# Multiply and tanh-GELU in two stretches of DRAM instead of three, with one multiply of 2048 columns on GpSimd

## The chip, the core and the metric

The kernel runs on one core of a Trainium2 chip. The metric is the device time of one execution in microseconds. Three runs of the kernel before took 119.83, 119.99 and 120.62 us; the median is 119.99.

## What is computed

Two arrays of 1024 x 4096 float32 (16.78 MB each) are multiplied element by element, and the product goes through the tanh form of GELU. The result has the same shape and type.

```python
z = x * y
return (0.5 * z * (1 + np.tanh(np.sqrt(2 / np.pi) * (z + 0.044715 * z ** 3)))).astype(np.float32)
```

Every element is independent of every other, so any cut of the arrays will do as long as x, y and the result are cut alike.

## The kernel before

The arrays are treated as flat memory. Split over the 128 partitions of SBUF, each array has 32768 columns of 4 bytes in every partition. The list `PIECES` (line 14) cuts the flat memory into three stretches, of 1280, 16384 and 15104 columns for each partition. Within a stretch, partition p holds one run of contiguous memory; `columns` (line 51) makes that view. So a row of a transfer, which is what one partition gets, is 5,120, 65,536 or 60,416 bytes of contiguous DRAM.

All of x stays in SBUF (`xs`, line 61, 128 KB for each partition). y does not fit beside it and has a smaller buffer, `ys` with `Y_BUF` = 20440 columns, in which later parts of y overwrite earlier ones. `Y_LOADS` (line 16) holds for each load of y its first and last column and its place in the buffer; `Y_FREE` (line 18) how many multiplies must be done before that load may be issued.

Everything in DRAM is moved by transfers that SyncE (SP) issues into one queue, in program order: x piece 0 and x piece 1 (moved by `_hoist` to the very front of the program), y load 0 (columns 1280 to 17664), x piece 2, then, after the third multiply, y load 1 (17664 to 32768), and after the fourth, y load 2 (0 to 1280). After these come three stores in the order of `STORES`. The first waits for y load 1 to have landed, and each waits for the activations of its own columns (lines 112 and 113). The waits stand in SP's program, so a wait that is not over holds back every later issue.

VectorE (DVE) multiplies in place, `xs = xs * ys` (line 96): four steps of 4096 columns, seven of 2048, one of 768 and one of 1280, as `STEPS` has them. It waits for the x and y that a step reads (lines 92 and 93), and each multiply adds one to `sem_mul`. ScalarE (ACT) applies the GELU in place (line 104), one activation for each multiply and in the same order; it waits for that multiply and adds one to `sem_act`. GpSimd (POOL) does no work of the kernel. At the end SP waits for the first two stores, clears the semaphores, and waits for the last store.

Of the kernel before, what the change touches and what calls it, by code (L numbers as in the profile page):

```python
# [1 line left out]

# [4 lines left out]


F32 = mybir.dt.float32
GELU = mybir.ActivationFunctionType.Gelu_apprx_tanh  # L10

PIECES = [(0, 1280), (1280, 17664), (17664, 32768)]

Y_LOADS = [(1280, 17664, 4056), (17664, 32768, 0), (0, 1280, 15104)]

Y_FREE = [0, 3, 4]

STEPS = [[4096] * 4, [2048] * 7 + [768], [1280]]  # L20
STORES = [(1280, 17664), (17664, 32768), (0, 1280)]
Y_BUF = 20440


def _hoist(nc, issued):

    here = nc.cur_bb.bb.instructions
    first = nc.main_func.blocks[0].instructions
    for ins in issued:
        del here[next(k for k, i in enumerate(here) if i is ins or i.name == ins.name)]  # L30
    engine = issued[0].engine
    at = next(
        k
        for k, i in enumerate(first)
        if i.engine == engine and type(i).__name__ == "InstDrain"
    )
    first[at:at] = issued


@with_exitstack  # L40
def kernel(
    ctx: ExitStack,
    tc: tile.TileContext,
    x: bass.AP,
    y: bass.AP,
    out: bass.AP,
):
    nc = tc.nc
    P = nc.NUM_PARTITIONS

    def columns(t, a, b):

        flat = t.flatten_outer_dims().rearrange("r c -> (r c)")
        pa, pb = next(q for q in PIECES if q[0] <= a and b <= q[1])
        return flat[P * pa : P * pb].rearrange("(p c) -> p c", p=P)[:, a - pa : b - pa]


    tc.close()
    tc.compile()  # L59

    xs = nc.alloc_sbuf_tensor("xs", [P, PIECES[-1][1]], F32).ap()
    ys = nc.alloc_sbuf_tensor("ys", [P, Y_BUF], F32).ap()
    sem_x = [nc.alloc_semaphore(f"sem_x{i}") for i in range(len(PIECES))]
    sem_y = [nc.alloc_semaphore(f"sem_y{i}") for i in range(len(Y_LOADS))]
    sem_mul = nc.alloc_semaphore("sem_mul")
    sem_act = nc.alloc_semaphore("sem_act")
    sem_o = [nc.alloc_semaphore(f"sem_o{i}") for i in range(len(STORES))]

    def load_x(i):
        a, b = PIECES[i]  # L70
        return nc.sync.dma_start(out=xs[:, a:b], in_=columns(x, a, b)).then_inc(sem_x[i], 16)

    def load_y(i):
        a, b, r = Y_LOADS[i]
        return nc.sync.dma_start(
            out=ys[:, r : r + b - a], in_=columns(y, a, b)
        ).then_inc(sem_y[i], 16)

    _hoist(nc, [load_x(0).ins, load_x(1).ins])
    load_y(0)  # L80
    load_x(2)
    for i in range(1, len(Y_LOADS)):
        if Y_FREE[i]:
            nc.sync.wait_ge(sem_mul, Y_FREE[i])
        load_y(i)

    n = 0
    done = {}
    for i, (a, b, r) in enumerate(Y_LOADS):
        for j, (xa, xb) in enumerate(PIECES):  # L90
            if xa <= a < xb:
                nc.vector.wait_ge(sem_x[j], 16)
        nc.vector.wait_ge(sem_y[i], 16)  # L93
        c = a
        for w in STEPS[i]:
            nc.vector.tensor_mul(  # L96
                out=xs[:, c : c + w],
                in0=xs[:, c : c + w],
                in1=ys[:, r + c - a : r + c - a + w],
            ).then_inc(sem_mul, 1)  # L100
            n += 1
            done[c + w] = n
            nc.scalar.wait_ge(sem_mul, n)
            nc.scalar.activation(  # L104
                out=xs[:, c : c + w], in_=xs[:, c : c + w], func=GELU
            ).then_inc(sem_act, 1)
            c += w

    for i, (a, b) in enumerate(STORES):
        if i == 0:  # L110
            nc.sync.wait_ge(sem_y[-2], 16)
        nc.sync.wait_ge(sem_act, done[b])
        nc.sync.dma_start(out=columns(out, a, b), in_=xs[:, a:b]).then_inc(sem_o[i], 16)
    for i in range(len(STORES) - 1):
        nc.sync.wait_ge(sem_o[i], 16)
    nums = sorted(s.num for s in [*sem_x, *sem_y, *sem_o[:-1], sem_mul, sem_act])
    assert nums == list(range(nums[0], nums[-1] + 1))
    nc.sync.sem_clear(range(nums[0], nums[-1] + 1))
    nc.sync.wait_ge(sem_o[-1], 16).then_inc(sem_o[-1], -16)


# [1 line left out]
_INS = ['x', 'y']  # L123
_OUTS = [((1024, 4096), 'float32')]


# [23 lines left out]
```

## Time and profile before

| what | value |
|---|---|
| median of three runs | 119.99 us |
| the profiled execution, its own time | 119.64 us |
| its span, first to last instruction | 118.3 us |
| HBM read, written | 33.55 MB, 16.78 MB |
| DVE busy | 35.2 us, 13 multiplies |
| ACT busy | 31.0 us, 13 activations and one table load |
| POOL busy | 0.2 us, four memsets |

The profile is that of one execution. Its span starts with the first instruction, SP's issue of x piece 0, and ends with SP's last wait; the time of the execution is 1.34 us longer. A row of the groups of instructions gives line, engine, operation, output and input with their shapes and count, then the busy time in us and the mean duration in ns, then the idle time ahead of the group and what ended it. The DMA bar cuts the span, or a window of it, into 40 equal slices; each digit is the share of the 16 DMA engines' time that was busy in a slice, in tenths. In a narrow window of that view a packet is put down where it starts, so that it shows the starts and not the busy time. The first half of the work begins on DVE at 42.45 us and the second at 78.12, each when a load of y has landed:

```profile
42.00:60.00 18.00, 17.43 (x4) 10.94 (x4) 0.00 (x0) 1.00 0.99 430
60.00:78.00 18.00, 0.00 (x0) 3.53 (x1) 0.00 (x0) 1.00 0.90 391
```

This is the table of windows: the stretch in us and its length, the busy time of DVE, ACT and POOL with the number of instructions, the granted TensorE clock (not used here), the DMA share, and GB/s.

### The profile page before, as it was taken

The page shows a single profiled execution, that of the slowest core. Times are in us where ns is not written, and L with a number is a line of the kernel's source. Part 1 is how long each engine was busy: PE and PEld are TensorE (multiplying, and loading weights), DVE is VectorE, ACT ScalarE, POOL GpSimd, SP SyncE. Part 2 cuts the span into 40 slices and gives each one's busy share as a digit, 9 for nine tenths or more (in the row PEclk, how much of TensorE's full clock was granted, in tenths as well). Part 3 has the DMA queues.
Part 4 walks back from the last instruction along what each step waited for, and adds up shares of the span by engine and source line. Part 5 has one row for each costly group of instructions (what it writes and reads, how often), then busy time and mean ns, then how long its engine had stood idle before and what let it go on. Part 6 is the DMA issues. An engine that isn't in the chain of part 4 may idle for free.

```text
span 118.3 us, 82 instructions
## 1 busy us (share of the span) xinstructions
DVE 35.2 (30%) x13; ACT 31.0 (26%) x14; POOL 0.2 (0%) x4
## 2 busy tenths in 40 slices
DVE  0000000000000069999920000059999940000000
ACT  3000000000000001977974000007998990000000
POOL 0000000000000000000000000000000000000000
DMA  9988899889988897797797797798899888977975
GB/s 375 556 355 355 355 643 421 355 355 421 643 355 355 355 654 327 327 654 327 327 654 327 327 654 327 327 576 355 355 576 487 355 355 368 613 327 327 654 327 222
DMA packets 1296, 50.33 MB, mean 425 GB/s; under 512 B 144, under 2 KB 144, under 8 KB 528
## 3 DMA queue, kind: packets, MB, share of 16 engines
q1 hardware_dynamic: 1296, 50.33, 98.8%
HBM read 33.55 MB, written 16.78 MB: 425 GB/s over the span
## 4 chain that ended last, share of the span: by engine, by line
DMA 53%; DVE 24%; ACT 3%; issue 1%; DVEq 0%
DMA ys<-in_y_dram 53%; DVE xs L96 24%; ACT xs L104 3%; DVEq L93 0%
## 5 line engine op out<-in xcount | busy, mean ns | idle before, releaser
L96 DVE TENSOR_TENSOR xs<-xs,ys 128x2048 f32<-128x2048 f32 (+3 forms) x13 | 35.2, 2778 | 60.7 <-DMA ys<-in_y_dram 60.7
L104 ACT ACTIVATE xs<-xs 128x2048 f32<-128x2048 f32 (+3 forms) x13 | 29.7, 2301 | 64.5 <-DVE xs L96 64.5
L104 ACT ACT_TABLE_LOAD x1 | 1.3, 1283 | 1.9 <-PEq L59 1.9
L134 POOL MEMSET const-bfloat16-1.0<- 128x1 bf16 x1 | 0.1, 102 | 0.0
L134 POOL MEMSET const-uint8-127<- 128x1 uint8 x1 | 0.1, 102 | 0.0
L134 POOL MEMSET const-float32-0.0<- 128x1 f32 x1 | 0.1, 99 | 0.2 <-issue 0.2
L134 POOL MEMSET const-float32-1.0<- 128x1 f32 x1 | 0.1, 99 | 0.0
## 6 DMA issues: line engine op xcount, KB each, us to landing
xs<-in_x_dram SPq DMA_DIRECT2D x1, 7552.0 KB, 57.9
ys<-in_y_dram SPq DMA_DIRECT2D x1, 7552.0 KB, 22.5
out_dram<-xs SPq DMA_DIRECT2D x1, 7552.0 KB, 20.4
xs<-in_x_dram SPq DMA_DIRECT2D x1, 640.0 KB, 3.6
ys<-in_y_dram SPq DMA_DIRECT2D x1, 640.0 KB, 19.7
out_dram<-xs SPq DMA_DIRECT2D x1, 640.0 KB, 20.8
xs<-in_x_dram SPq DMA_DIRECT2D x1, 22.6
ys<-in_y_dram SPq DMA_DIRECT2D x1, 40.4
```

Source lines behind the costliest of these rows:

```text
L96: nc.vector.tensor_mul(out=xs[:, c : c + w], in0=xs[:, c : c + w], in1=ys[:, r + c - a : r + c - a + w],).then_inc(sem_mul, 1)
L104: nc.scalar.activation(out=xs[:, c : c + w], in_=xs[:, c : c + w], func=GELU).then_inc(sem_act, 1)
L134: nc = _bacc.Bacc("TRN2", target_bir_lowering=False, num_devices=1)
```

## The change

The stretches of DRAM become two, of 16384 columns each, so that all views of DRAM have a distance of 64 KB from row to row. What is loaded is cut apart from them: x as columns 0 to 1280 (heads of the rows of stretch 0, 5 KB each), 1280 to 16384 and 16384 to 32768; y as 0 to 16384, 16384 to 31488 and, as tails of the rows of stretch 1, 31488 to 32768. There are two stores, one for each stretch, each with rows of 64 KB, and the last columns no longer have a store to themselves.

The first half is multiplied in four steps of 4096 columns, as before. The second half is cut into nine: 1024, 2048 and 2048 columns, then 2048 that GpSimd multiplies, then the tail of 1280, three of 2048 and one of 1792. GpSimd has a semaphore of its own, `sem_pool`. ACT takes the steps in the order of the list, GpSimd's as the fourth of the second half. A step now waits for every load of x that it touches, and the clear at the end has the new semaphore in its range.

```diff
-PIECES = [(0, 1280), (1280, 17664), (17664, 32768)]
+PIECES = [(0, 16384), (16384, 32768)]
+X_LOADS = [(0, 1280), (1280, 16384), (16384, 32768)]
...
-Y_LOADS = [(1280, 17664, 4056), (17664, 32768, 0), (0, 1280, 15104)]
+Y_LOADS = [(0, 16384, 4056), (16384, 31488, 0), (31488, 32768, 15104)]
...
-STEPS = [[4096] * 4, [2048] * 7 + [768], [1280]]
-STORES = [(1280, 17664), (17664, 32768), (0, 1280)]
+STEPS = [
+    *((0, c, 4096, False) for c in range(0, 16384, 4096)),
+    (1, 16384, 1024, False),
+    (1, 17408, 2048, False),
+    (1, 19456, 2048, False),
+    (1, 21504, 2048, True),
+    (2, 31488, 1280, False),
+    *((1, c, min(2048, 31488 - c), False) for c in range(23552, 31488, 2048)),
+]
+STORES = PIECES
...
+    waited = {nc.vector: set(), nc.gpsimd: set()}
+    muls = {nc.vector: 0, nc.gpsimd: 0}
+    sem_of = {nc.vector: sem_mul, nc.gpsimd: sem_pool}
+    for i, c, w, on_pool in STEPS:
+        engine = nc.gpsimd if on_pool else nc.vector
+        needed = [sem_y[i]] + [
+            sem_x[j] for j, (xa, xb) in enumerate(X_LOADS) if xa < c + w and c < xb
+        ]
+        for sem in needed:
+            if sem.num not in waited[engine]:
+                waited[engine].add(sem.num)
+                engine.wait_ge(sem, 16)
+        a, b, r = Y_LOADS[i]
+        engine.tensor_mul(
+            out=xs[:, c : c + w],
+            in0=xs[:, c : c + w],
+            in1=ys[:, r + c - a : r + c - a + w],
+        ).then_inc(sem_of[engine], 1)
+        muls[engine] += 1
+        nc.scalar.wait_ge(sem_of[engine], muls[engine])
+        nc.scalar.activation(
+            out=xs[:, c : c + w], in_=xs[:, c : c + w], func=GELU
+        ).then_inc(sem_act, 1)
...
-        nc.sync.wait_ge(sem_act, done[b])
+        nc.sync.wait_ge(sem_act, max(n for n, (_, c, _, _) in enumerate(STEPS, 1) if a <= c < b))
```

More of the change, by code (lines that the diff above doesn't have):

```diff
@@ L62 @@
     ys = nc.alloc_sbuf_tensor("ys", [P, Y_BUF], F32).ap()
-    sem_x = [nc.alloc_semaphore(f"sem_x{i}") for i in range(len(PIECES))]
+    sem_x = [nc.alloc_semaphore(f"sem_x{i}") for i in range(len(X_LOADS))]
     sem_y = [nc.alloc_semaphore(f"sem_y{i}") for i in range(len(Y_LOADS))]
     sem_mul = nc.alloc_semaphore("sem_mul")
+    sem_pool = nc.alloc_semaphore("sem_pool")
     sem_act = nc.alloc_semaphore("sem_act")
@@ L69, in load_x @@
     def load_x(i):
-        a, b = PIECES[i]
+        a, b = X_LOADS[i]
         return nc.sync.dma_start(out=xs[:, a:b], in_=columns(x, a, b)).then_inc(sem_x[i], 16)
@@ L85 @@
         load_y(i)
[L87 to L107, printed above, removed]
+    waited = {nc.vector: set(), nc.gpsimd: set()}
[21 more added lines that the diff above has]
+        ).then_inc(sem_act, 1)
     for i, (a, b) in enumerate(STORES):
@@ L115 @@
         nc.sync.wait_ge(sem_o[i], 16)
-    nums = sorted(s.num for s in [*sem_x, *sem_y, *sem_o[:-1], sem_mul, sem_act])
+    nums = sorted(s.num for s in [*sem_x, *sem_y, *sem_o[:-1], sem_mul, sem_pool, sem_act])
     assert nums == list(range(nums[0], nums[-1] + 1))
```

## The prediction

> **What bounds the kernel now.** I read the page's head, its DMA bar and its queue row first.
>
> ```profile
> span 118.3 us, 82 instructions
> DMA  9988899889988897797797797798899888977975
> q1 hardware_dynamic: 1296, 50.33, 98.8%
> ```
>
> The bar never falls to a gap; the queue's packets fill 98.8% of sixteen engines' span. DVE (35.2 us) and ACT (31.0 us) are idle two thirds of it. The kernel ends when 50.33 MB have moved; compute matters only if it leaves the queue empty.
>
> So I looked for unused queue time. At the front, the DMA view of 0 to 4 us (slices of 0.1 us):
>
> ```profile
> DMA  0000000000993956798979799969999990000000
> ```
>
> The first packet starts in the eleventh slice, at about 1.04 us, although SyncE issued at 0.00: **issue to first packet is 1.04 us**. At the end, the issue rows give the three stores' times to landing (the row without a size is the 8,192 KB store), and SyncE's timeline their issues, the last two in windows of their own:
>
> ```profile
> out_dram<-xs SPq DMA_DIRECT2D x1, 7552.0 KB, 20.4
> out_dram<-xs SPq DMA_DIRECT2D x1, 640.0 KB, 20.8
> out_dram<-xs SPq DMA_DIRECT2D x1, 20.9
> ...
> 96.33 0.34 SPq L113 DMA_DIRECT2D out_dram<-xs  x1
> 97.49 0.33 SPq L113 DMA_DIRECT2D out_dram<-xs  x1
> ```
>
> They land at 78.04 + 20.9 = 98.9, 96.33 + 20.4 = 116.7 and 97.49 + 20.8 = 118.3. The DMA view of 98 to 99 us (slices of 25 ns) holds sixteen packets of 60 KB, one for each engine: the second store's first ones.
>
> ```profile
> DMA  0000000000009999999900000000000000000000
> ```
>
> They start between 98.3 and 98.5 us. That is when the engines finish store 0, so **the next store must be issued by 98.3 - 1.04 = 97.3 us** or the queue runs dry. Now it is issued at 96.33: 0.9 us to spare. The work that releases it, the chain of waits and two shape rows:
>
> ```profile
> 78.03 0.03 issue
> 78.06 0.02 DVEq L93
> 78.08 0.04 issue
> 78.12 1.52 DVE xs L96
> 79.64 0.69 issue
> 80.33 13.31 DVE xs L96 x6
> 93.64 0.02 issue
> 93.66 3.80 ACT xs L104 x3
> ...
> L96 DVE TENSOR_TENSOR xs<-xs,ys 128x2048 f32<-128x2048 f32 x7 | 15.5, 2286 | 18.2 <-DMA ys<-in_y_dram 18.2
> L104 ACT ACTIVATE xs<-xs 128x2048 f32<-128x2048 f32 x7 | 13.4, 1910 | 18.7 <-DVE xs L96 18.7
> ```
>
> From the second large y load (78.03) it is DVE back to back, then ACT. The 0.69 us of "issue" is no gap: the first multiply lasts 2.29 us, so it covers them.
>
> **What the Trainium skill says.** "SBUF — State Buffer", Who interferes with whom: a DVE instruction with two SBUF inputs contends with a GpSimd instruction that reads SBUF, since DVE's second input comes through the read interface that both share; the section calls it an exclusive lock, and "SBUF: two separate sides" adds that the later one is blocked until the earlier is through. Every multiply here has two SBUF inputs. The trace before cannot agree or differ: POOL has four memsets, over by 0.5 us. Its other rule, that compute and DMA do not slow each other, fits: while DVE and ACT worked, 80 to 98 us, the DMA share was 0.94. "DMA: Bandwidth & Descriptors", Latency and other measured facts, gives 207 GB/s per direction at a row pitch of 512 KiB, where larger powers of two fall to half; 64 KB is below these. The trace agrees: the large x and y loads of the first 42 us have that pitch and moved at full rate.
>
> **The change, part by part.**
>
> *Transfers.* The bytes stay; nine transfers become eight, and a third of the 384 rows of 5 KB goes. The last store of such rows adds 118.3 - 116.7 = 1.6 us for 0.655 MB; at the stream's 50.33 MB / (118.3 - 1.04 - 0.4) = 431 GB/s it would be 1.52. At most 0.1 us is gained. The x heads at 64 KB pitch are the first packets of all; bounds -0.3 to +0.3 us, since the first stretch to 42.4 us lost 0.4 us against 431 GB/s; I take 0.
>
> *First half.* The first multiply waits for 16.78 MB instead of 17.43: 1.5 us earlier. SyncE's y1 and y2 (waits on the third and fourth multiply) move from 55.57 and 59.91 to some 54.0 and 58.4. The transfer before y1 still ends near 60 (x2 now 2.30 + 57.9 = 60.2), so this slack only grows: worth 0. Three waits ahead of DVE's first multiply cost one 0.02 us event more, hidden by the wait for y0.
>
> *Second half, no contention.* y1 lands after the same bytes, at 78.03; y2 and store 0 queue behind it as before. ACT's starts give the step between DVE multiplies: 2.20 us for 2048 columns, 4.33 for 4096, so 0.07 us + 1.04 ns a column, and a result 0.08 after the next start. ACT takes 0.20 us + 0.83 ns a column, with 0.095 of overlap (1.91 + 0.83 + 1.25 in 3.80). DVE from 78.12: the 1024 columns done at 79.33, then 81.54, 83.74, the 1280 tail at 85.14, and 87.34, 89.54, 91.74, 93.68. **The GpSimd multiply is not in the trace.** The skill's price, "GPSIMD Engine Reference", Elementwise — side-by-side cycle accounting, is 4,497 ns for an fp32 add of 2048 (and 2,293 for DVE, where this trace has 2,286, which lends it weight). I bound a multiply between 2.3 us (DVE's rate) and twice the price, 9 us. At 4.5 it is done at 82.6. ACT takes it fourth, and is not free before 85.6. From there ACT is back to back: 87.5, 88.7, 90.5, 92.3, 94.1, 95.73. Store 1 is issued at 95.75, **1.5 us before the deadline: nothing is lost**. Store 1 now waits for all of its half, without the 1280 columns that a third store took later; were DVE alone to do it, its end at 95.88 would put ACT's at 97.6, 0.3 late.
>
> *Second half, with the lock.* DVE and POOL are released together; nothing in the trace says who starts first, and I let DVE win. Its 1024 columns end at 79.3, POOL runs 4.5 with about 0.1 on each side, DVE resumes at 83.95. The seven left end at 98.37. Behind DVE's multiply stand six more, and behind its wait all of ACT: ACT's fourth to ninth then end at 100.42, store 1 is issued at 100.44, its first packet comes at 101.48, and the sixteen engines have stood still since 98.3 to 98.5: **3.1 us lost**. If POOL wins, the same sum gives 3.0. From 101.48, 8.39 MB at 431 GB/s take 19.5, landing 0.4: span 121.3, where it was 118.3. SyncE's final waits and its clear of the semaphores lie beside the last store. Nothing else stands in POOL's queue.
>
> Bounds of the contention: below, 0 (the queue cannot be fuller than 98.8%); above, POOL held until DVE's last multiply.
>
> **The rivals.**
>
> 1. *Lock, one side held for the other's whole instruction:* +3.0. For it: the skill, and the same shared second input. Against: no measurement here. **0.40.**
> 2. *No loss* (the other side): POOL works beside DVE, or DVE loses less than 1.8 us. Price 0 to -0.1; it decides as long as the store is issued by 97.3, so with POOL done by 87.1 or DVE under about 12% slower. For it: 1.5 us of slack. **0.37.**
> 3. *The interface is shared in turn,* DVE 15 to 25% slower: ACT ends at 97.7 to 99.3, +0.5 to +2.1, I take 1.6. **0.10.**
> 4. *POOL starves* because DVE's multiplies overlap: POOL done at 98.3, ACT stuck at its fourth, end 108.4: +11. **0.10.**
> 5. *Faster by over 1%:* 1.2 us would have to come out of a stream that idles only 1.04 + 0.4 us, neither touched. **0.03.**
>
> That the change doesn't do what it says: its loads and stores are plainly issued so; only POOL's being beside DVE is open, and that is rival 1, 3 or 4.
>
> **The numbers.** The profiled execution took 119.64 us, 1.34 more than its span; the median, 119.99, is 0.35 above it. The likeliest case is the lock: 119.99 + 3.05 = **123.0** (span 121.3, own range 122.3 to 123.6, POOL 3.8 to 5 us). No loss gives 119.9. The range from 119.5 to 123.6 holds rivals 1, 2 and 3 but their fringes, 0.83 in all. Faster by over 1%, 0.03; within 1% (about 1.2 us, what a measurement of this kernel can tell from no change), 0.37; slower, 0.60, from rivals 1, 3 and 4.
>
> **What would show it.** With the lock: store 1 issued near 100.4, zeros in the DMA bar for 3 us after 98.4, DVE idle or one multiply of some 6.5 us near 79 to 84, and POOL's multiply about 4.5 us of work. Right but for the size: the same hole with another width. Wrong: multiplies of 2.29 us on DVE throughout, ACT ending near 95.7, store 1 issued before 97.3 and a closed DMA bar. Starvation: POOL's multiply ending after DVE's last, ACT waiting for it from 85.6.

## The result

The changed kernel takes 122.69 us (median of five runs, 122.60 to 122.95); the kernel before took 119.95 beside it. The ratio is 1.0232, 95% interval 1.0204 to 1.0260: slower by 2.7 us. The forecast was 123.0 with a range of 119.5 to 123.6, and slower as the likeliest side. The profiled execution took 122.60 us, its span is 121.3.

The page of the changed kernel, the lines that answer to those of before:

```profile
span 121.3 us, 82 instructions
...
DMA  6977977977997899779979979699777908897778
...
q1 hardware_dynamic: 1152, 50.33, 96.7%
```

The same 50.33 MB now fill 96.7% of a longer span, and the bar has what it never had before: a 0, in the 33rd slice, which covers 97.0 to 100.1 us. (A packet of 64 KB counts where it starts, and store 0's last ones started at 96.4 to 96.7, so no start falls into that slice though they moved until 99.0; the hole is bounded below with finer views.) The groups of instructions, shapes apart:

```profile
L110 DVE TENSOR_TENSOR xs<-xs,ys 128x2048 f32<-128x2048 f32 x5 | 15.5, 3143 | 0.0
L117 ACT ACTIVATE xs<-xs 128x2048 f32<-128x2048 f32 x6 | 11.1, 1898 | 5.8 <-DVE xs L110 5.8
L110 POOL TENSOR_TENSOR xs<-xs,ys 128x2048 f32<-128x2048 f32 x1 | 5.5, 5542 | 78.3 <-DMA ys<-in_y_dram 78.3
```

DVE's mean for 2048 columns rose from 2286 to 3143 ns. A mean hides which one it was, so here is the timeline (start, duration) from the landing of the second large y load, DVE's second multiply taken by itself from a narrow window, and POOL's:

```profile
78.64 0.35 SPq L125 DMA_DIRECT2D out_dram<-xs  x1
...
78.65 7.74 DVE L110 TENSOR_TENSOR xs<-xs,ys 128x1024 f32<-128x1024 f32 x2 [19.77 <-DMA ys<-in_y_dram]
78.69 5.54 POOL L110 TENSOR_TENSOR xs<-xs,ys 128x2048 f32<-128x2048 f32 x1 [78.26 <-DMA ys<-in_y_dram]
...
79.79 6.60 DVE L110 TENSOR_TENSOR xs<-xs,ys 128x2048 f32<-128x2048 f32 x1
...
86.42 1.91 ACT L117 ACTIVATE xs<-xs 128x2048 f32<-128x2048 f32 x1 [5.46 <-DVE xs L110]
```

One multiply took the whole loss: 6.60 us where the others take 2.28. Neither engine shows as idle; the wait for the other is inside the recorded duration. POOL ends at 78.69 + 5.54 = 84.23 and DVE's long multiply at 79.79 + 6.60 = 86.39, 2.16 us later: nearly all of its own work came after POOL's end. And POOL, recorded from 78.69, worked only from the end of DVE's first multiply (79.88): 4.35 us.

What that does to the store, in SyncE's timeline and the DMA view of 98 to 103 us (slices of 0.125 us, a packet put down at its start):

```profile
100.51 0.34 SPq L125 DMA_DIRECT2D out_dram<-xs  x1
...
DMA  0000000000000000000000000099000000000000
```

Store 1 is issued at 100.51, and its sixteen first packets start between 101.25 and 101.5. Store 0's closing packets, small ones of which each engine has one, lie between 98.9 and 99.1; from 99.1 to 101.2 no packet starts at all. The hole is about 2.4 us.

That is not all of the 3.0 us of span. The second y load landed at 78.63, not 78.03, after the same number of bytes: 0.6 us went earlier, in the loads. The row of DMA issues for the first 640 KB, in the change and then in the kernel before, shows where it begins:

```profile
xs<-in_x_dram SPq DMA_DIRECT2D x1, 640.0 KB, 4.1
```

```profile
xs<-in_x_dram SPq DMA_DIRECT2D x1, 640.0 KB, 3.6
```

The first transfer, now the 5 KB heads at a distance of 64 KB, took 4.1 us to land; the contiguous 640 KB of before took 3.6. The chain of waits shows that nothing more was lost later. Its lines for the two large y loads (start and length, so the sum is the landing), kernel before first:

```profile
1.93 40.42 DMA ys<-in_y_dram
...
55.57 22.46 DMA ys<-in_y_dram
```

```profile
1.91 39.51 DMA ys<-in_y_dram
...
54.57 24.05 DMA ys<-in_y_dram
```

Between the two landings the kernel before takes 35.7 us for 15.47 MB, the change 37.2 us for 16.12 MB: 433 GB/s both times, so the distance of 64 KB does not slow the stream. The 0.6 us is lost ahead of the first landing, which came 0.9 us earlier than before where 0.66 MB less should have brought 1.5.

### The profile page after: what moved, and what is told of

It reads as the page before. It is cut to its first block, busy times and chain, and to the rows that moved or that the text cites. A ratio compares the mean times of both kernels' runs of the same rounds, so it can differ in the third digit from the quotient of the medians.

```text
span 121.3 us, 82 instructions
## 1 busy us (share of the span) xinstructions
DVE 37.3 (31%) x12; ACT 30.6 (25%) x14; POOL 5.7 (5%) x5
## 2 busy tenths in 40 slices
DMA packets 1152, 50.33 MB, mean 415 GB/s; under 512 B 128, under 2 KB 128, under 8 KB 384
## 3 DMA queue, kind: packets, MB, share of 16 engines
q1 hardware_dynamic: 1152, 50.33, 96.7%
## 4 chain that ended last, share of the span: by engine, by line
DMA 52%; DVE 19%; ACT 10%; issue 0%
DMA ys<-in_y_dram 52%; DVE xs L110 19%; ACT xs L117 10%
## 5 line engine op out<-in xcount | busy, mean ns | idle before, releaser
L110 DVE TENSOR_TENSOR xs<-xs,ys 128x2048 f32<-128x2048 f32 (+4 forms) x12 | 37.3, 3176 | 61.2 <-DMA ys<-in_y_dram 61.2
L117 ACT ACTIVATE xs<-xs 128x2048 f32<-128x2048 f32 (+4 forms) x13 | 29.3, 2296 | 68.0 <-DVE xs L110 68.0
L110 POOL TENSOR_TENSOR xs<-xs,ys 128x2048 f32<-128x2048 f32 x1 | 5.5, 5542 | 78.3 <-DMA ys<-in_y_dram 78.3
```

The costliest lines, as they stand in the source:

```text
L110: engine.tensor_mul(out=xs[:, c : c + w], in0=xs[:, c : c + w], in1=ys[:, r + c - a : r + c - a + w],).then_inc(sem_of[engine], 1)
L117: nc.scalar.activation(out=xs[:, c : c + w], in_=xs[:, c : c + w], func=GELU).then_inc(sem_act, 1)
```

## The experiments

**GpSimd taken out of the changed kernel.** Everything else stays, so this divides the loss between GpSimd and the layout.

```diff
-    (1, 21504, 2048, True),
+    (1, 21504, 2048, False),
```

> The changed kernel with GpSimd's multiply given back to DVE, same place in the order, nothing else. Theory (DVE is held for GpSimd's whole multiply): all multiplies of 2048 columns take 2.28 us, the last activation ends near 98.1 us in the span (second y load at 78.65 plus 19.5), store 1 is issued near 98.2 and its first packets come near 99.1, just as the engines finish store 0 (98.9 to 99.1): no hole in the DMA stream or one under 0.3 us. Span 118.9 to 119.3, time 120.2 to 120.7. Rival (the new layout of rows and the two stores cost the time, GpSimd does not): time stays at 122.4 to 122.9.

Measured: 120.49 us, ratio to the kernel before 1.0054 (1.0035 to 1.0073). Its timeline of the second half and the DMA view of 98 to 103 us:

```profile
78.95 17.77 DVE L110 TENSOR_TENSOR xs<-xs,ys 128x1024 f32<-128x1024 f32 x9 [19.77 <-DMA ys<-in_y_dram]
...
98.47 0.34 SPq L125 DMA_DIRECT2D out_dram<-xs  x1
...
DMA  0000000000990000000000000000009900000000
```

DVE does 2048 columns more and is through in 17.77 us, where it took 19.89 with help. Store 1 is issued 19.53 us after the y load instead of 21.87, and its packets start at 99.25 to 99.5 as the engines finish store 0, whose closing packets lie between 99.19 and 99.31: a gap of some 0.15 us is left of the hole. So GpSimd costs 2.0 to 2.2 us (122.69 - 120.49 = 2.2; 2.0 with each taken against the kernel before beside it, 119.95 and 119.75), and the rest of the change about 0.7.

**The multiply on GpSimd where DVE is idle.** The helper stays, and only the place moves: the last 2048 columns of the first half, after DVE's last multiply of that half.

```diff
-    *((0, c, 4096, False) for c in range(0, 16384, 4096)),
+    *((0, c, 4096, False) for c in range(0, 12288, 4096)),
+    (0, 12288, 2048, False),
+    (0, 14336, 2048, True),
...
-    (1, 21504, 2048, True),
+    (1, 21504, 2048, False),
...
+        if on_pool:
+            engine.wait_ge(sem_mul, 4)
```

> GpSimd still multiplies 2048 columns, but those at the end of the first half, and only after DVE's last multiply of that half, when DVE is idle for some 20 us. Theory: GpSimd's multiply takes about 4.4 us, all multiplies of 2048 on DVE take 2.28 us, and the time is that of the kernel without GpSimd (within 0.3 us). Rival (a GpSimd multiply costs the kernel some 2 us wherever it stands, by its start or by slowing DMA): 122 us or more.

Measured: 120.38 us, ratio 1.0050 (1.0032 to 1.0068), the same as without GpSimd. The rows of the two engines:

```profile
L114 DVE TENSOR_TENSOR xs<-xs,ys 128x2048 f32<-128x2048 f32 x7 | 15.7, 2283 | 0.0
...
L114 POOL TENSOR_TENSOR xs<-xs,ys 128x2048 f32<-128x2048 f32 x1 | 4.5, 4507 | 56.7 <-DVE xs L114 56.7
```

Alone, the multiply takes 4.51 us, and no DVE multiply is stretched. So a GpSimd multiply by itself costs this kernel nothing that shows; it costs by standing beside DVE's.

**Which access holds.** Two kernels with all multiplies on DVE give GpSimd an extra instruction on unused columns of `ys` when the y load lands: one fills them (no input), one copies them (one input).

```diff
-    (1, 21504, 2048, True),
+    (1, 21504, 2048, False),
...
+    nc.gpsimd.wait_ge(sem_mul, 4)
+    nc.gpsimd.wait_ge(sem_y[1], 16)
+    nc.gpsimd.memset(ys[:, 16384:18432], 0.0).then_inc(sem_pool, 1)
...
+    nc.sync.wait_ge(sem_pool, 1)
```

> All multiplies on DVE, and GpSimd fills 2048 unused columns of ys with zeros from the moment the second y load has landed: an instruction that writes SBUF and reads nothing, extra work. Theory (the lock is on the shared read interface): no multiply on DVE is longer than 2.3 us, time as the kernel without GpSimd within 0.4 us. Rival (any GpSimd instruction on SBUF holds DVE): one DVE multiply longer by the fill's own duration, some 1.8 us or more, and the end later by about that.

In the second kernel the fill is replaced:

```diff
+    nc.gpsimd.tensor_copy(out=ys[:, 18432:20440], in_=ys[:, 16384:18392]).then_inc(sem_pool, 1)
```

> All multiplies on DVE, and GpSimd copies 2008 unused columns of ys to others from the moment the second y load has landed: one SBUF input, extra work. Theory (an instruction that reads SBUF holds the shared interface for its whole length): one DVE multiply is longer by the copy's working time (some 1.8 to 3 us), and store 1 comes later by that less what slack there is. Rival (DVE and GpSimd share the interface in turn, by bandwidth): several DVE multiplies each longer by some tenths, none doubled; with one input instead of two for GpSimd the loss is at most half of that with the multiply.

Measured, one run each: 120.66 us with the fill, 122.60 with the copy. The fill's rows, then the copy's with DVE's second multiply from the timeline:

```profile
L110 DVE TENSOR_TENSOR xs<-xs,ys 128x2048 f32<-128x2048 f32 x6 | 13.4, 2284 | 0.0
...
L123 POOL MEMSET ys<- 128x2048 f32 x1 | 1.8, 1805 | 78.7 <-DMA ys<-in_y_dram 78.7
```

```profile
L110 DVE TENSOR_TENSOR xs<-xs,ys 128x2048 f32<-128x2048 f32 x6 | 15.0, 2555 | 0.0
...
L123 POOL COPY ys<-ys 128x2008 f32<-128x2008 f32 x1 | 2.8, 2829 | 79.0 <-DMA ys<-in_y_dram 79.0
...
80.45 3.94 DVE L110 TENSOR_TENSOR xs<-xs,ys 128x2048 f32<-128x2048 f32 x1
```

The fill lies beside DVE for 1.8 us and changes nothing. The copy adds six times 2555 - 2284 ns, 1.6 us, to DVE's multiplies. They are one multiply again: its record is 3.94 us, the others keep 2.28. So it is GpSimd's reading that holds DVE, as far as one run of each shows. The copy holds it for less than the multiply, 1.66 against 4.32 us, and a little less than the 1.8 expected at least; from the end of DVE's first multiply (80.54) to its own end (82.25) it has 1.7 us, so the hold is again the length of GpSimd's work. Counted from the y load, store 1 is issued after 21.2 us, where the fill has 19.5 and the change 21.9. The kernel is as late as the change all the same, because its y load landed 0.7 us later in this run.

**Size of the hold.** GpSimd's share is halved.

```diff
-    (1, 21504, 2048, True),
+    (1, 21504, 1024, True),
+    (1, 22528, 1024, False),
```

> The changed kernel, GpSimd's multiply cut to 1024 columns, the other 1024 on DVE. Theory (hold as long as GpSimd's instruction): DVE's second multiply takes 2.28 plus some 2.2 us, store 1 is issued near 99.3, hole about 1.1 us, time about 121.4 to 121.8, near the middle between the change and the kernel without GpSimd. Rival (a fixed cost of starting GpSimd, whatever its size): DVE's second multiply near 6.6 us and the time near 122.5.

Measured: 121.97 us in one run, 0.2 above what was expected at most; its second half began at 79.26, late like the other runs with heads. DVE's second multiply, and SyncE's issue of store 1:

```profile
80.40 4.44 DVE L111 TENSOR_TENSOR xs<-xs,ys 128x2048 f32<-128x2048 f32 x1
...
99.88 0.34 SPq L126 DMA_DIRECT2D out_dram<-xs  x1
```

The stretch is 4.44 - 2.28 = 2.16 us, half of 4.32. From the y load to the store it takes 20.63 us, between 19.53 without GpSimd and 21.87 with 2048 columns. The cost goes with GpSimd's columns; no fixed price for starting it shows.

**Who gets the interface next.** The same 2048 columns as two multiplies.

```diff
-    (1, 21504, 2048, True),
+    (1, 21504, 1024, True),
+    (1, 22528, 1024, True),
```

> The changed kernel, GpSimd's 2048 columns as two multiplies of 1024. Theory (the hold lasts for one instruction, and whoever waits gets the interface next): DVE and GpSimd alternate; two DVE multiplies of 2048 are longer by 2.2 us each (about 4.4 us), the second GpSimd multiply also waits for a DVE multiply and shows 4 us or more; store 1 as late as in the change or some 0.2 us later, time 122.5 to 123.2. Rival (GpSimd keeps the interface as long as it has work queued): one DVE multiply of about 6.7 us and none of 4.4.

Measured: 123.06 us in one run. DVE's third multiply and GpSimd's second, each from a narrow window:

```profile
84.52 4.43 DVE L111 TENSOR_TENSOR xs<-xs,ys 128x2048 f32<-128x2048 f32 x1
...
82.40 4.41 POOL L111 TENSOR_TENSOR xs<-xs,ys 128x1024 f32<-128x1024 f32 x1
```

GpSimd's second multiply begins at 82.40, waits for DVE's second one (which ends at 84.60) and ends at 86.81, with 2.2 us of its own work; DVE's third is stretched for that time. In this run they take turns, an instruction each. DVE loses 2.16 + 2.15 us, as with one long multiply.

**The hold in the kernel before.** Three stretches, three stores, and one step on GpSimd.

```diff
+ON_POOL = [25856]
...
-            nc.vector.tensor_mul(
+            engine, sem = (nc.gpsimd, sem_pool) if c in ON_POOL else (nc.vector, sem_mul)
+            engine.tensor_mul(
...
-            ).then_inc(sem_mul, 1)
+            ).then_inc(sem, 1)
```

> The kernel before with its three stretches and three stores, and only its fifth step of 2048 columns of the second half multiplied on GpSimd. Theory (the hold): DVE's second multiply of the half takes about 6.7 us instead of 2.28 (GpSimd waits for the first, then works 4.5 us), ACT runs back to back from there and ends its twelfth activation near 99.6, store 1 is issued near 99.7 instead of 96.3, first packets near 100.6, a hole of some 2.1 us after 98.4: time 121.6 to 122.1. Rival (without two stores and the new rows GpSimd helps or does nothing): 119.5 to 120.1.

Measured: 121.82 us, ratio 1.0165 (1.0140 to 1.0189). DVE's second multiply and the page's row of GpSimd:

```profile
80.97 6.60 DVE L102 TENSOR_TENSOR xs<-xs,ys 128x2048 f32<-128x2048 f32 x1
...
L102 POOL TENSOR_TENSOR xs<-xs,ys 128x2048 f32<-128x2048 f32 x1 | 6.6, 6607 | 78.4 <-DMA ys<-in_y_dram 78.4
```

The same stretched multiply, the same loss of some 2 us, without two stores and without the new rows. GpSimd's own record is longer here, 6.6 against 5.5 us, only because DVE's first multiply, for which it waits, has 2048 columns and not 1024.

**The layout by itself.** Without GpSimd, x is loaded as two whole stretches, so that no 5 KB heads come first.

```diff
-X_LOADS = [(0, 1280), (1280, 16384), (16384, 32768)]
+X_LOADS = [(0, 16384), (16384, 32768)]
...
-    _hoist(nc, [load_x(0).ins, load_x(1).ins])
+    _hoist(nc, [load_x(0).ins])
...
-    load_x(2)
+    load_x(1)
```

> The kernel without GpSimd's multiply, and x loaded as its two whole stretches (64 KB rows), so that the 5 KB heads with a 64 KB distance are gone from the start. Theory (the heads' slow first packets delay every later load by 0.4 to 0.6 us): both halves start at 40.9 to 41.2 and 78.0 to 78.4 instead of 41.75 and 78.95, time 119.8 to 120.1, as before. Rival (the 64 KB distance as such slows the whole stream): no gain, 120.4 or more, with the time between the loads' landings longer than in the kernel before.

Measured: 120.33 us, ratio 1.0041 (1.0027 to 1.0055). The first half starts at 41.25 instead of 41.75, just outside what was expected, the second only at 78.72 instead of 78.95, and the time gained, 0.16 us, is within the two intervals. The expectation was a miss. The rival's cause fails too, though its 120.4 us was nearly met. At the rate of before, the 16.12 MB between the landings of the two large y loads take 37.2 us; eight of the nine profiles of the new layout have 37.20 to 37.23, and only this kernel's has 37.5. The layout loses its time ahead of the first landing: at the rate of before it would come at 40.8 us; it came at 41.4 to 42.1 in the seven profiles with heads and at 41.2 and 41.3 in this kernel and the next.

**A version meant to beat both.** As the last one, and the second half's steps are seven of 2048, the tail of 1280 and at last 768 columns, all on DVE.

```diff
-    (1, 16384, 1024, False),
-    (1, 17408, 2048, False),
-    (1, 19456, 2048, False),
-    (1, 21504, 2048, True),
+    *((1, c, 2048, False) for c in range(16384, 30720, 2048)),
     (2, 31488, 1280, False),
-    *((1, c, min(2048, 31488 - c), False) for c in range(23552, 31488, 2048)),
+    (1, 30720, 768, False),
```

> A version meant to beat both: no heads, no GpSimd, two stores, and the second half multiplied in seven steps of 2048, the 1280 tail and last 768, so that the end of ACT comes soon after DVE's. Theory: ACT ends near 96.9, store 1 is issued by 97.0, before store 0 is through at 98.4 less 0.9: no hole; time 119.5 to 119.9 (0 to 0.3 us under the kernel before, which the two transfers' worth of small rows less is at most). If the first packets of 64 KB rows start slower than the 5 KB rows of before: 120.0 or more.

Measured: 120.13 us, ratio 1.0032 (1.0022 to 1.0042): better than the change, 0.35 us slower than the kernel before, and a miss by the first expectation. Store 1 was issued at 97.90, soon enough: its first packets follow store 0 at 98.8. What is lost is lost at the start, where the expectation's second sentence had it: the DMA view of its 0 to 4 us (slices of 0.1 us) shows sixteen first packets, from 1.0 us on, and not one second packet before 4.0.

```profile
DMA  0000000000999909999000000000000000000000
```

At the 431 GB/s of the stream before, one of sixteen engines takes 2.4 us for a 64 KB packet; the second ones would have begun from 3.4 us. They began between 4.0 and 4.7, 3.0 us after the first ones on average, so each engine lost some 0.6 us.

## Why the prediction was right

**The mechanism** was the one forecast: DVE first, GpSimd held until DVE's first multiply ends, then DVE held for GpSimd's whole multiply. The likeliest case was 123.0 us, 0.3 from the measured time, at a chance of 0.40. The range held no loss as well, so a time inside it would tell little; the stretched multiply and the hole tell. The hold is shown from several sides: it vanishes without GpSimd and with GpSimd beside an idle DVE; it stays in the kernel before; it goes with GpSimd's columns (2.16 and 4.32 us for 1024 and 2048); it comes with a reading instruction and not with a filling one. This agrees with what the Trainium skill ("SBUF — State Buffer", Who interferes with whom) says of two SBUF inputs and of instructions that only write, though no run here has a DVE instruction with a single SBUF input, so the need for two on DVE's side is not shown; the price of "GPSIMD Engine Reference", 4,497 ns, was measured as 4,507.

**The rivals.** No loss fell with the 6.60 us multiply. Sharing in turn fell too: one multiply is stretched and the rest keep 2.28 us. Starvation fell: GpSimd got the interface at the first boundary between two DVE multiplies, though DVE's next one was queued.

**The sum was right for partly wrong reasons.** Two terms were off and nearly cancelled: 0.6 us lost in the loads and a hole of 2.4 us make the 3.0 us of span, where the forecast had 0 and 3.1. That they cancelled was luck.

*The heads, taken as 0 between -0.3 and +0.3.* The y load that starts the second half was 0.6 us late, outside the bounds. The seven profiles with heads first have 4.1 to 4.7 us to the landing of the first 640 KB, the two with the contiguous 640 KB 3.6 and 3.5. The change without GpSimd is 0.74 us slower than the kernel before in the medians. I had looked at the distance of 64 KB in full stream and taken it for harmless; the first packets after a start are another matter.

*The hole, taken as 3.1 us.* It measured 2.4. Store 1's issue was nearly exact, 100.51 against 100.44, but from two errors: 0.6 late at the start, and 0.5 less work after it, mainly since the hold was 4.3 us and not 4.5 with 0.1 on either side. The late y load makes the hole neither larger nor smaller, since store 0 is late with it: it ended at about 99.0 and not 98.4, 20.4 us after the y load in both. What made the hole smaller is the 0.5 us less work, and that store 1's first packets came 0.8 to 1.0 us after its issue and not 1.04, the figure from the start of the program.

**DVE alone** was put 0.3 us past the deadline. Counted from the y load, that sum was right: store 1 was to be issued after 19.6 us and was after 19.53. It left only some 0.15 us because its packets began 0.87 us after the issue and not 1.04.

**Open.** The landings put the layout's loss at the start of the program, where both kinds of rows 64 KB apart have slow first packets. Why they are slow is not known, nor why the first landing differs by up to 0.6 us among the profiles with heads. Taking the heads away regained only 0.16 us in the medians, and that kernel's profile has 0.25 us more between the landings than the other eight; the cause is open. (The kernel before with GpSimd has 0.4 us more there than the kernel before, but its profile is of the slowest of its four executions.) Other first loads than these three kinds were not tried.

## What to carry to other kernels

Moving work from DVE to GpSimd did not help while DVE ran instructions with two SBUF inputs: 2048 columns took 2.2 us off DVE and put 4.3 us of holding on it. Put a GpSimd instruction that reads SBUF where DVE is idle, or leave it on DVE; and where two engines can hold each other, look for one recorded duration far above its group's mean, not for idle time. In a kernel that lives from a full DMA queue, work out by when the next transfer must be issued and count every stretch of compute against that time.

## What was not expected of the hardware

The first packets of the program are slow in a way that depends on the rows: the 640 KB landed 3.5 to 3.6 us after the issue as one contiguous block and 4.1 to 4.7 us as 5 KB rows 64 KB apart, and with 64 KB rows at the start the first packets took 3.0 us on average, where the stream's take 2.4. The hand-over between GpSimd and DVE shows no cost in these records: DVE's held multiply ended 2.16 us after GpSimd's, and an undisturbed one has a record of 2.28 us.
